# Three tiles of the ConvFFN up projection get other SBUF places: a kernel for one diffusion-transformer layer

## The chip, the cores and the metric

The kernel runs on one core of one Trainium2 chip. The metric is the device time of one execution of the program in microseconds (us). It is compared by the median of several executions.

A few names are used throughout. PE is the matrix engine, DVE the vector engine, ACT the scalar engine, POOL the GpSimd engine, and SP the engine whose queue issues most of the transfers between SBUF (the on-chip memory that all engines read) and DRAM. PSUM is the memory that PE writes its sums to. Each engine works through its own list of instructions in order. An instruction that waits holds up everything behind it on its engine.

## The reference

One layer of a diffusion backbone on 1024 latent tokens of width 1024, in float32. Two attention branches are mixed and added to the residual, a layer norm follows, and then a convolutional feed-forward block. The change lies in the last part, so only that is shown:

```
def _conv_ffn(h, w_up, conv_w, conv_b, w_down):
    u = h @ w_up                                  # (1024 x 1024) @ (1024 x 5632)
    u = depthwise convolution of width 3 along the tokens (u) + conv_b
    gate, val = split(u, 2)                       # 2816 columns each
    return (silu(gate) * val) @ w_down            # (1024 x 2816) @ (2816 x 1024)
...
h = x * (1 + scale2) + shift2
x = layer_norm(DEEPNORM_ALPHA * x + gate2 * _conv_ffn(h, ...))
```

The result must keep float32 accuracy.

## The kernel before, in words

**Layout.** Everything is held transposed: 128 channels on the partitions, the 1024 tokens along the free dimension. Each float32 operand of a large product is split into a high and a low part (`split`, L78: ACT casts the high part, another engine subtracts it for the low part). One product is then three matmuls per 128 channels: high by high, high by low, low by high (`mm3`, L87 to L90).

**Stages.** Modulation and projections come first, then attention, then the output projection with the first layer norm. After that come the up projection with convolution and gating (`up_conv` and `up_tile`), the down projection, and the last layer norm. The up projection has 22 column tiles j of 128 gate and 128 value channels.

**The first three tiles** (j = 0, 1, 2, `NCL = 3`) are done by `up_conv` (L1275) as plain products of the normed activations `B{f}_{half}`. Each gives two PSUM tiles, `u0_j` for the gate and `u1_j` for the values. `conv3` (L1232) turns them into SBUF tiles `c0_j` and `c1_j` with one pass of ACT and two of DVE. ACT applies the Silu to `c0_j` (L1286). `gated` (L1242) multiplies the two on DVE (L1245), forms the sum of the two token halves in the first half of `c1_j` (L1246), and has SP store three pieces to the DRAM tile `td[j]`: the two halves of `c0_j` (L1247, L1248), and the sum from `c1_j`, written twice (L1249).

**The other nineteen tiles** are done by `up_tile` (L1360) with a two-by-two block algorithm that needs seven block products in place of eight (Strassen's form). For tile j these are, in the order in which PE does them: A11 (into bank a), S2 (b), S1 (c), S3 (d), A12 (a), S4 (c), A22 (d). Each is 12 matmuls of 512 columns per bank, so a tile is 84 matmuls. S1 to S4 are sums of weight blocks. The activations need sums too: T1 to T4 (table `prods`, L1228). They are made once, before tile 3, by `build(k)` (L1108) for k = 0 to 3:

- `s1` and `s2` form the sums `t13_k` and `t24_k` in the four-buffer ring `tm`, partly on DVE and partly on POOL
- ACT casts `t13_k` to the high part `T13h_k` and `t24_k` to `T24h_k` (L1115), and DVE makes the low parts `T13l_k` and `T24l_k` (L1116, recorded at the helper's line L1077)

S2 multiplies by T2 and thus by all four `T24h_k` and `T24l_k`, k = 0 to 3 in turn. S1 and S3 use the T13 tiles. In the trace the names have no numbers, so `b<-T24h,wS` is a matmul of S2.

**Where tiles lie.** 35 SBUF places of 4 KB per partition (`H0` to `H18` and `Z0` to `Z15`) are handed out by `ht` (L131) from the front of a list, `hfree`, and given back to its end by `hput` (L135). This happens while the program is written, not while it runs. A place that is given back and taken again makes the new tile's first writer wait until the old tile's last reader is done. Where the old tile is stored to DRAM, that last reader is the transfer, so the wait is for its landing.

**Order of the work.** PE's list is written out by hand in program order. On the other engines a scheduler orders the instructions from the dependences that it sees, so a different place for a tile can move instructions there. The build steps are interleaved with `up_conv` (each waits its turn in the list `pend`).

In `up_conv` before the change, the slot of `c1_j` goes back to the list right after `gated`, while its store is still to come. With the list as short as it is there, these two places are taken again at once:

| Place | Tile before it | Taken next, before | Taken next, after |
|---|---|---|---|
| Z14 | c1_1 (its sum is stored to td[1]) | T24h_2 | tv3 |
| H7 | z1_0 (free early) | T24l_2 | T24h_2 |
| H3 | v1 (free early) | c1_2, then T24h_3 | T24l_2 |
| H18 | z3_0 (read last by build(3)) | T24l_3 | T24h_3 |
| Z2 | v3 (read last by build(3)) | pv3 | T24l_3 |
| Z1 | B3_1 (read by the plain products) | pv4 | c1_2, then pv4 |
| Z12, H17, H5 | B0_1, B1_1, B2_1 | ug3, uv3, tv3 | pv3, ug3, uv3 |

`c1_2` held H3 before, so that `T24h_3` had to wait for the landing of the store of `c1_2`. Later tiles keep the same rotation under other names of places, up to the end of the kernel.

Of the kernel before, what the change touches and what calls it, by code (L numbers as in the profile page):

```python
# [40 lines left out]
NCL = 3  # L41
# [26 lines left out]
def layer_kernel(  # L68
# [59 lines left out]
    hfree = [(hp, f"H{n}") for n in range(19)]  # L128
    hslot = {}

    def ht(name, shape=(P, T), dt=F32):  # L131
        hslot[name] = pool, tag = hfree.pop(0)
        return pool.tile(list(shape), dt, tag=tag, name=name, bufs=1)

    def hput(*names):  # L135
        for n in names:
            hfree.append(hslot.pop(n))
# [741 lines left out]
    def tm(name, dt=F32, w=T):  # L879
        return post.tile([P, w], dt, tag="m", name=name, bufs=4)  # L880
# [22 lines left out]
    def hsl(hf):  # L903
        return slice(hf * HALF, (hf + 1) * HALF)
# [37 lines left out]
    for f in range(2, KT):  # L942
# [4 lines left out]
        for j in range(4):  # L947
            k = (f % 2) * 4 + j
# [59 lines left out]
    def drain(keep=0):  # L1008
        while len(pend) > keep:
            pend.pop(0)[1]()  # L1010
            clock[0] = 0.0
# [64 lines left out]
    def sub(e, o, a, b, op=ALU.subtract):  # L1076
        e.tensor_tensor(out=o, in0=a, in1=b, op=op)  # L1077
# [30 lines left out]
    def build(k):  # L1108
        (b11, b21), (b12, b22) = [[z[:, a] for a in (0, 1)] for z in (zt_[k, 0], tp["v", k])]
        st = {}  # L1110

        def parts(a, e):
            for p in "hl":
                tp[a + p, k] = ht(f"T{a}{p}_{k}", (P, 2, HALF), R32)
            nc.scalar.copy(tp[a + "h", k], st[a])  # L1115
            sub(e, tp[a + "l", k], st[a], tp[a + "h", k].bitcast(F32))  # L1116

        def s1():
            st["13"] = t = tm(f"t13_{k}").rearrange("p (a q) -> p a q", a=2)
            sub(nc.vector, t[:, 1], b12, b11)  # L1120
            sub(nc.gpsimd, t[:, 0], b22, b12)

        def s2():
            st["24"] = t = tm(f"t24_{k}").rearrange("p (a q) -> p a q", a=2)
            sub(nc.vector, t[:, 1], b22, st["13"][:, 1])
            sub(nc.gpsimd if k % 2 else nc.vector, t[:, 0], b21, t[:, 1])
            hput(f"z{k}_0", f"v{k}")

        return [s1, s2, lambda: parts("13", nc.vector), lambda: parts("24", nc.vector)]
# [102 lines left out]
    def conv3(t, u, c):  # L1232
        nc.scalar.activation(t, u, AF.Identity, bias=cvb[:, c:c + 1], scale=cvw[:, c, 1:2])
        nc.vector.scalar_tensor_tensor(out=t[:, 1:T], in0=u[:, 0:T - 1], scalar=cvw[:, c, 0:1], in1=t[:, 1:T],
                                       op0=ALU.mult, op1=ALU.add)
        nc.vector.scalar_tensor_tensor(out=t[:, 0:T - 1], in0=u[:, 1:T], scalar=cvw[:, c, 2:3],
                                       in1=t[:, 0:T - 1], op0=ALU.mult, op1=ALU.add)
# [4 lines left out]
    def gated(j, tg, tv):  # L1242
        lo, hi = tg[:, 0:HALF], tg[:, HALF:T]
        if j < NH:
            nc.vector.tensor_tensor(out=tg, in0=tg, in1=tv, op=ALU.mult)  # L1245
            nc.vector.tensor_tensor(out=tv[:, 0:HALF], in0=lo, in1=hi, op=ALU.add)  # L1246
            nc.sync.dma_start(td[j][:, 0], lo)  # L1247
            nc.sync.dma_start(td[j][:, 3], hi)  # L1248
            nc.sync.dma_start(td[j][:, 1:3], twice(tv[:, 0:HALF]))  # L1249
        else:  # L1250
            nc.vector.scalar_tensor_tensor(out=tg, in0=tg, scalar=-1.0, in1=tv, op0=ALU.mult, op1=ALU.mult)
            nc.sync.dma_start(g2d[j - NH], tg)
            nc.gpsimd.dma_start(td[j - NH][:, 2:4], twice(hi), accum_op=ALU.add)
# [8 lines left out]
    def up_mm(j, gv, slices):  # L1262
        ps, w, done = up_start(j, gv)
        for s in slices:
            if s.start in done:
                continue
            done.add(s.start)
            hf = s.start // HALF
            c = slice(s.start - hf * HALF, s.stop - hf * HALF)
            for k in range(KT):  # L1270
                t = tp["B", k, hf]
                mm3(ps[:, s], (w[0][:, k], w[1][:, k]), (t[:, 0, c], t[:, 1, c]), k == 0, k == KT - 1)
                tick((s.stop - s.start) / 0.8)

    def up_conv(j):  # L1275
        cv = []
        for gv in (0, 1):
            up_mm(j, gv, [hsl(0), hsl(1)])
            if gv == 0:
                hslot[f"c0_{j}"] = pool, tag = cs[j % 2]  # L1280
                t = pool.tile([P, T], F32, tag=tag, name=f"c0_{j}", bufs=1)
            else:
                t = ht(f"c1_{j}")
            conv3(t, ups.pop((j, gv))[0], gv * NF + j)
            cv.append(t)
        nc.scalar.activation(cv[0], cv[0], AF.Silu)  # L1286
        gated(j, *cv)
        hput(f"c1_{j}")

    up_weights(1, 0, 1)  # L1290
    up_weights(1, 1, 1)
# [8 lines left out]
    cs = [hfree.pop(0) for _ in range(2)]  # L1300
    for k in range(4):
        pend += [(BLD, fn) for fn in build(k)]
    for j in range(NCL):
        up_conv(j)
    drain()
    hput(*[f"B{k}_1" for k in range(4)])


    ps3.release()
# [429 lines left out]
```

## Time and profile before

| What | Value |
|---|---|
| Median of 3 runs | 1600.66 us (1598.8 to 1603.46) |
| Profiled execution, its own time | 1605.64 us |
| Its span, first to last instruction | 1603.9 us |
| Time of that execution outside the span | 1.74 us |
| Mean granted clock of PE | 0.991 |
| PE busy | 1538.9 us, 96% of the span |
| DVE, ACT, POOL busy | 74%, 51%, 46% |

The profile is of one execution. Its time of 1605.64 us is 4.98 us over the median of the three runs and 2.18 us over the slowest of them. In a row of the timeline the first number is the start in us from the beginning of the span, the second the length, then engine, line, operation, output and inputs. Brackets at the end give the idle time of the engine just before it and who ended that. The view of waits gives for each pair of instruction and releaser the total wait, how often, and the longest. The view by windows gives busy time of each engine in a stretch, with the granted clock of PE as a share of full speed.

### The profile page before, as it was taken

To read this page: it belongs to the slowest core of one execution; us is meant where nothing else is said; L and a number is where in the kernel's file an instruction comes from. 1 tells how busy PE (TensorE), PEld (TensorE's weight loads), DVE (VectorE), ACT (ScalarE), POOL (GpSimd) and SP (SyncE) were. 2 spreads that over 40 slices of the span, in tenths; PEclk is the share of its full clock that TensorE was granted. 3 is DMA by queue.
4 is the path that set the end of the run, shared out by engine and by line. 5 is a ranking of instruction groups with operands and counts; after the bars stand their busy time and mean duration, and the time that the engine had idled before them with its cause. 6 is when DMAs were issued, how large, how long until landed. Compare 5 with 4: busy or idle time off the path is not lost.

```text
span 1603.9 us, 22190 instructions
## 1 busy us (share of the span) xinstructions
PE 1538.9 (96%) x7748; PEld 1278.2 (80%) x7748; DVE 1180.8 (74%) x1768; ACT 813.6 (51%) x1450; POOL 730.7 (46%) x727
## 2 busy tenths in 40 slices
PE   6999999999998999999999999899999999999997
PEld 5878788888877887777688987688888888888887
DVE  7797646628887777888684788588888788656884
ACT  5422222448887667688431564344544444435552
POOL 0673202426666556665422454366667665021021
PEclk9999999999999999999999999999999999999999
DMA  9695662322236565531451223233334446996831
GB/s 378 225 315 185 199 211 84 118 83 65 61 114 142 137 134 136 122 74 33 164 168 41 79 80 105 93 106 105 105 106 105 106 113 175 354 286 207 260 108 53
DMA packets 112368, 230.00 MB, mean 143 GB/s; under 512 B 12960, under 2 KB 27808, under 8 KB 112160
## 3 DMA queue, kind: packets, MB, share of 16 engines
q1 hardware_dynamic: 96816, 198.93, 37.5%
q0 software_dynamic: 10400, 20.19, 8.3%
q10 hardware_dynamic: 5040, 9.46, 1.6%
q8 instruction: 61, 1.00, 0.3%
q14 instruction: 51, 0.42, 0.1%
HBM read 177.35 MB, written 65.86 MB: 152 GB/s over the span
## 4 chain that ended last, share of the span: by engine, by line
PE 77%; DVE 10%; ACT 4%; DMA 4%; issue 4%; POOL 2%; SPq 0%; DVEq 0%; ACTq 0%; POOLq 0%
PE ptr L529 5%; PE p L88 4%; PE p L89 4%; PE p L90 4%; PE g L88 2%; PE g L89 2%; PE g L90 2%; PE s L412 2%; PE av L550 2%; PE b L90 2%; PE b L89 2%; PE c L88 2%; PE c L89 2%; PE c L90 2%; PE b L88 2%
## 5 line engine op out<-in xcount | busy, mean ns | idle before, releaser
L539 DVE TENSOR_TENSOR ptl<-ptr,pth 128x512 fp32r<-128x512 f32 x188 | 124.6, 684 | 30.0 <-ACT pth L538 27.8
L529 PE MATMUL ptr<-ident,p 128*128 128x128 f32 x816 | 127.7, 279 | 11.6 <-DVE ptl L539 6.8
L538 ACT CAST pth<-ptr 128x512 fp32r<-128x512 f32 x188 | 106.6, 588 | 58.0 <-PE ptr L529 32.8
L85 DVE TENSOR_TENSOR ld<-rd,hd 128x1024 fp32r<-128x1024 f32 x77 | 94.8, 1249 | 50.0 <-ACT hd L80 44.9
L424 ACT ACTIVATE p<-p,nm 128x1024 f32<-128x1024 f32 (+2 forms) x128 | 125.3, 981 | 11.1 <-DVE p L457 10.3
L529 PEld LDWEIGHTS ptr<-ident,p 128*128 128x128 f32 x816 | 94.5, 141 | 42.1 <-DVE ptl L539 13.6
L80 ACT CAST hd<-rd 128x1024 fp32r<-128x1024 f32 x77 | 79.4, 1050 | 81.9 <-PE p L90 55.1
L550 PE MATMUL av<-pth,VT 128*128 128x512 f32 x236 | 104.9, 445 | 1.0 <-ACT avs L556 0.5
L88 PE MATMUL p<-hd 128*128 128x512 f32 x264 | 103.2, 391 | 0.0
L89 PE MATMUL p<-ld,hd 128*128 128x512 f32 x264 | 102.8, 390 | 0.0
L90 PE MATMUL p<-hd,ld 128*128 128x512 f32 x264 | 102.8, 389 | 0.0
L90 PE MATMUL g<-hh,wlg 128*128 128x512 f32 x256 | 99.8, 390 | 0.5 <-POOL wlg L85 0.5
L88 PE MATMUL g<-hh,whg 128*128 128x512 f32 x256 | 99.9, 390 | 0.0
L89 PE MATMUL g<-hl,whg 128*128 128x512 f32 x256 | 99.6, 389 | 0.0
L551 PE MATMUL av<-ptl,VT 128*128 128x512 f32 x236 | 97.8, 415 | 1.8 <-POOL ptl L85 1.8
L85 POOL TENSOR_TENSOR wlg<-wg,whg 128x512 fp32r<-128x512 f32 x32 | 44.1, 1385 | 115.0 <-ACT whg L80 115.0
L457 DVE TENSOR_SCALAR_CACHE_REDUCE p<-s,cvt,nmc 128x1024 f32<-128x1024 f32 x64 | 84.4, 1339 | 12.7 <-PE s L413 12.0
L412 PE MATMUL s<-KL,q 128*128 128x512 f32 (+2 forms) x192 | 76.3, 397 | 2.9 <-ACT p_x L424 2.0
L186 DVE CUSTOM_DVE_ANT_0 wml<-wml,sc,bmc 128x1024 f32<-128x1024 f32 x32 | 47.0, 1478 | 42.7 <-DMA wml<-in_wmodT_dram 40.8
L413 PE MATMUL s<-KL,q 128*128 128x512 f32 (+2 forms) x192 | 71.9, 375 | 0.0
L80 ACT CAST wS<-s 128x512 fp32r<-128x512 f32 x76 | 45.8, 621 | 50.0 <-POOL s L1077 45.8
L82 POOL TENSOR_SCALAR pth<-prw 128x512 fp32r<-128x512 f32 x48 | 31.1, 649 | 87.5 <-ACT prw L535 62.2
(420 smaller groups left out, 4955.9 us busy)
## 6 DMA issues: line engine op xcount, KB each, us to landing
wml<-in_wmodT_dram SPq DMA_DIRECT2D x48, 512.0 KB
ru<-in_w_up_dram SPq DMA_DIRECT2D x38, 512.0 KB
rd<-td SPq DMA_DIRECT2D x55, 256.0 KB
rd<-sd SPq DMA_DIRECT2D x44, 256.0 KB
rd<-in_w_dn_dram SPq DMA_DIRECT2D x33, 256.0 KB
wm<-in_wmodT_dram SPq DMA_DIRECT2D x16, 512.0 KB
wg<-in_w_g_dram SPq DMA_DIRECT2D x32, 256.0 KB
sgd<-sg ACTq DMA_DIRECT2D x32, 256.0 KB
```

The source lines that it names most:

```text
L80: nc.scalar.copy(hi, src)
L85: lo_eng.tensor_tensor(out=lo, in0=src, in1=hi.bitcast(F32), op=ALU.subtract)
L88: nc.tensor.matmul(ps, a[0], b[0], start=start, stop=False, skip_group_check=resumed)
L89: nc.tensor.matmul(ps, a[0], b[1], start=False, stop=False, skip_group_check=resumed)
L90: nc.tensor.matmul(ps, a[1], b[0], start=False, stop=stop, skip_group_check=resumed)
L412: nc.tensor.matmul(o, self.q[0][:, hs], ks, start=True, stop=False)
L424: nc.scalar.activation(p, s, AF.Exp, bias=nm[:, h:h + 1], scale=scale, accum_out=sm[:, h:h + 1])
L529: nc.tensor.transpose(tr[:, h * P:(h + 1) * P], self.pslice(h, n), ident)
L538: nc.scalar.copy(hi, tr)
L539: nc.vector.tensor_tensor(out=lo, in0=tr, in1=hi.bitcast(F32), op=ALU.subtract)
L550: nc.tensor.matmul(self.av, v, hi, start=first, stop=False)
L551: nc.tensor.matmul(self.av, v, lo, start=False, stop=self.left == 0)
```

## The change

It has three edits, all in the placing of tiles. First, before `c1_2` is placed, the place of `B3_1` is given back and put at the front of the list, so that `c1_2` takes it. Second, the places of `c1_1` and `c1_2` aren't given back after `gated`, but after the whole stage. Third, at the end of the stage only `B0_1` to `B2_1` are still given back, and then `c1_1` and `c1_2`. The place of `c1_0` is given back at once as before.

```
             else:
+                if j == NCL - 1:
+                    hput("B3_1")
+                    hfree.insert(0, hfree.pop())
                 t = ht(f"c1_{j}")
...
         gated(j, *cv)
-        hput(f"c1_{j}")
+        if j:
+            later.append(f"c1_{j}")
+        else:
+            hput(f"c1_{j}")
...
+    later = []
     for j in range(NCL):
         up_conv(j)
     drain()
-    hput(*[f"B{k}_1" for k in range(4)])
+    hput(*[f"B{k}_1" for k in range(3)], *later)
```

No instruction is added or removed, and the lists of PE and SP stay as they were. ACT, DVE and POOL get another order in one stretch, the end of `up_conv` and the first steps of tile 3.

ACT before, from the Silu of tile 1's gate to the cast of `T24h_2`. `wS1_3` is the weight operand S1 of tile 3, `s12_3` and `s34_3` are the weight sums that POOL makes, and what an instruction waits for stands in brackets (`DMAHW6` is a transfer queue's count).

```order
L1286 ACTIVATE c0_1_10226<-c0_1_10226 128x1024 [waits DVE_49,Activation_49]
L1115 CAST T13h_3_10461<-t13_3_10455 128x1024 [waits DVE_49,Pool_49]
L1233 ACTIVATE c1_1_10293<-u1_1_10230,cvt_70 128x1024 [waits DMAHW7_49,DMAHW0_49,PE_49]
L80 CAST wS1_3_10497<-s12_3_10485 128x512 [waits Pool_49]
L80 CAST wS2_3_10494<-s12_3_10485 128x512 [waits Pool_49]
L80 CAST wS3_3_10500<-s34_3_10486 128x512 [waits Pool_49]
L80 CAST wA12_3_10551<-ru0_3_10481 128x512 [waits PE_49]
L1233 ACTIVATE c0_2_10372<-u0_2_10309,cvt_70 128x1024 [waits DMAHW2_49,DMAHW1_49,PE_49]
L1115 CAST T24h_2_10432<-t24_2_10404 128x1024 [waits DMAHW6_49,DVE_49,Activation_49]
```

ACT before, a little later, around the cast of `T24h_3`. The row `pv3` is the first copy that follows product A11 of tile 3.

```order
L1233 ACTIVATE c1_2_10445<-u1_2_10382,cvt_70 128x1024 [waits PE_49]
L80 CAST wA11_4_10584<-ru0_4_10560 128x512 [waits DMAHW0_49]
L1368 COPY pv3_10507<-a3_10503 128x512 [waits PE_49]
L80 CAST wS2_4_10617<-s12_4_10564 128x512 [waits Pool_49]
L1115 CAST T24h_3_10465<-t24_3_10458 128x1024 [waits DMAHW3_49,DVE_49,Activation_49]
L80 CAST wS1_4_10620<-s12_4_10564 128x512 [waits PE_49]
```

ACT now, from the same Silu:

```order
L1289 ACTIVATE c0_1_10226<-c0_1_10226 128x1024 [waits DVE_49,Activation_49]
L1115 CAST T24h_2_10432<-t24_2_10404 128x1024 [waits DVE_49]
L1115 CAST T13h_3_10461<-t13_3_10455 128x1024 [waits DVE_49,Pool_49]
L1233 ACTIVATE c1_1_10293<-u1_1_10230,cvt_70 128x1024 [waits DMAHW7_49,DMAHW0_49,PE_49]
L80 CAST wS1_3_10497<-s12_3_10485 128x512 [waits Pool_49]
L1115 CAST T24h_3_10465<-t24_3_10458 128x1024 [waits Pool_49]
L80 CAST wS2_3_10494<-s12_3_10485 128x512 [waits Pool_49]
L80 CAST wS3_3_10500<-s34_3_10486 128x512
L80 CAST wA12_3_10551<-ru0_3_10481 128x512 [waits PE_49]
L1233 ACTIVATE c0_2_10372<-u0_2_10309,cvt_70 128x1024 [waits DMAHW2_49,DMAHW1_49,PE_49]
```

`T24h_2` moves ahead by seven rows and `T24h_3` by eleven, and neither waits for a transfer any more. `T24h_3` waits for POOL alone, that is for the half of `t24_3` that POOL makes.

DVE, the difference from the sum `t13_3` to the low part of the weight operand A11 of tile 3 (`wA11_3`), the first operand that PE needs there:

```order
 L1077 TENSOR_TENSOR t13_3_10455<-v3_9945,z3_0_9083 128x512
+L1077 TENSOR_TENSOR T24l_2_10433<-t24_2_10404,T24h_2_10432 128x1024
+L1077 TENSOR_TENSOR T24l_1_10363<-t24_1_10334,T24h_1_10362 128x1024
+L1234 SCALAR_TENSOR_TENSOR c1_1_10293<-u1_1_10230,cvt_70,c1_1_10293 128x1023
+L1077 TENSOR_TENSOR t24_3_10458<-v3_9945,t13_3_10455 128x512
+L1236 SCALAR_TENSOR_TENSOR c1_1_10293<-u1_1_10230,cvt_70,c1_1_10293 128x1023
+L1077 TENSOR_TENSOR T13l_3_10462<-t13_3_10455,T13h_3_10461 128x1024
+L1245 TENSOR_TENSOR c0_1_10226<-c0_1_10226,c1_1_10293 128x1024
+L1077 TENSOR_TENSOR T24l_3_10466<-t24_3_10458,T24h_3_10465 128x1024
+L1246 TENSOR_TENSOR c1_1_10293<-c0_1_10226 128x512
 L85 TENSOR_TENSOR wA11_3_10491<-ru0_3_10481,wA11_3_10491 128x512
```

Before, `wA11_3` stood right behind `t13_3`. Now nine rows stand between them. Behind `wA11_3` follow the low parts of S2, S1, S3 and A12 of tile 3 in one run, and then the convolution of `c0_2`. Before, `T24l_2` stood inside that convolution, and `T24l_3` behind the low part of tile 4's S2.

On POOL three rows change places: the sums `s12_3` (first half), `s34_3` (first half) and `t24_3` now come in this order, with the second half of `s12_3` after them. Before, both halves of `s12_3` came first, then `t24_3`, then `s34_3`. The first half of `s12_3` waited for DVE's `T24l_1` before and waits for `T24l_2` now, since their `tm` buffers are reused.

Two waits for transfers are new in the later rows: the first writer of `tv3` waits for the store of `c1_1` (its place was Z14), and the copy to `pv4` on ACT waits for the store of `c1_2` (Z1).

## The prediction

> **What bounds the kernel now.** I read the page first, then the view by windows around the end of `up_conv`, the waits there, PE's timeline, and the chain of waits that ends last.
>
> ```profile
> span 1603.9 us, 22190 instructions
> PE 1538.9 (96%) x7748; PEld 1278.2 (80%) x7748; DVE 1180.8 (74%) x1768; ACT 813.6 (51%) x1450; POOL 730.7 (46%) x727
> core 0: us, PE busy (x) PEld busy (x) DVE busy (x) ACT busy (x) POOL busy (x), PEclk, DMA share, GB/s
> 964.00:998.00 34.00, 34.00 (x151) 28.15 (x150) 26.91 (x27) 14.63 (x18) 15.64 (x10) 1.00 0.31 108
> 998.00:1010.00 12.00, 4.54 (x16) 3.11 (x15) 7.03 (x7) 2.33 (x4) 1.54 (x2) 0.83 0.39 131
> 1010.00:1024.00 14.00, 14.00 (x57) 11.36 (x57) 4.07 (x6) 4.76 (x8) 4.72 (x4) 0.90 0.12 39
> 1024.00:1354.00 330.00, 330.00 (x1458) 273.25 (x1457) 279.91 (x252) 159.89 (x226) 219.93 (x127) 1.00 0.40 112
> 1354.00:1550.00 196.00, 196.00 (x869) 161.51 (x868) 136.64 (x141) 97.83 (x107) 36.67 (x29) 1.00 0.82 254
> ```
>
> PE bounds the kernel: it is busy for 96% of the span. From 1024 to 1550 us it has no idle time at all, at full granted clock. In 998 to 1010 it works 4.54 of 12 us, and there and in the next stretch its clock is 0.83 and 0.90. So there is one hole, and whatever closes it moves all behind it ahead. The waits of the stretch 964 to 1024 and the chain name the cause:
>
> ```profile
> POOL s L1077 <- DVE T24l L1077: 15.2, 1, 15.2
> ACT T24h L1115 <- DMA td<-c: 9.7, 2, 6.8
> PE b L88 <- ACT T24h L1115: 7.0, 1, 7.0
> ...
> 996.57 1.11 ACT c L1233
> ...
> 1000.09 1.21 DVE c L1236
> ...
> 1001.32 1.24 DVE c L1245
> ...
> 1003.48 3.22 DMA td<-c
> ...
> 1006.79 1.05 ACT T24h L1115
> ...
> 1007.87 1.24 DVE T24l L1077
> ...
> 1009.15 0.80 PE b L89
> ```
>
> Read upwards: PE's product S2 of tile 3 waits for `T24h_3`, ACT's cast for the landing of `c1_2`'s store out of the same place H3, and that store for the whole convolution of tile 2, which can't start before PE has finished `u1_2`. The operand itself was long ready. Two casts waited for stores: the longer wait, 6.8 us, is `T24h_3`; the other is `T24h_2`, for which PE did not wait.
>
> **What the change takes away.** PE's own rows give the size of the hole:
>
> ```profile
> 995.98 0.39 PE L88 MATMUL a<-B,wA 128*128 128x512 f32 x1
> ...
> 998.70 0.39 PE L88 MATMUL b<-T24h,wS 128*128 128x512 f32 x1
> ...
> 1000.51 0.39 PE L90 MATMUL b<-T24h,wS 128*128 128x512 f32 x1
> 1007.89 0.79 PE L88 MATMUL b<-T24h,wS 128*128 128x512 f32 x1 [6.99 <-ACT T24h L1115]
> 1009.15 0.80 PE L89 MATMUL b<-T24l,wS 128*128 128x512 f32 x1 [0.47 <-DVE T24l L1077]
> ...
> 1011.45 0.63 PE L88 MATMUL c<-T13h,wS 128*128 128x512 f32 x1
> 1011.87 0.63 PE L89 MATMUL c<-T13l,wS 128*128 128x512 f32 x1
> ...
> 1025.07 0.39 PE L88 MATMUL a<-B,wA 128*128 128x512 f32 x1
> ```
>
> - Product A11's 12 matmuls take 998.70 − 995.98 = 2.72 us, so one starts every 0.227 us.
> - Tile 3 begins at 995.98 and tile 4 at 1025.07, which is 29.09 us for 84 matmuls. At 0.227 they take 19.04. The hole costs **10.05 us**.
> - Of these, 7.15 are standing still: the next start would have been 1000.51 + 0.23 = 1000.74, and it came at 1007.89.
> - The other 2.90 come after it: 0.47 of waiting for `T24l_3`, and starts 0.42 us apart (1011.45 to 1011.87) until the granted clock is back.
>
> The clock term rests on those rows. The Trainium skill, "TensorE: Matmul & The Clock Gate", Part 1, says that PE falls to half its clock after an idle window of about 3.4 us and needs as long a busy one to come back. By that page the tail would be 1.7 us (half of 3.4) and the wait of 0.47, so that the hole would be worth about 9.3 us and the estimate would end near 1591.3. I keep the measured 10.05.
>
> **Is the new operand there in time?** The rest depends on when the four moved rows finish now. These rows of before carry the estimate:
>
> ```profile
> 971.97 1.06 ACT L1286 ACTIVATE c<-c 128x1024 f32<-128x1024 f32 x1 [4.83 <-DVE c L1236]
> 974.30 1.05 ACT L1115 CAST T13h<-t 128x1024 fp32r<-128x1024 f32 x1 [1.27 <-DVE t L1077]
> 975.26 1.20 ACT L1233 ACTIVATE c<-u,cvt 128x1024 f32<-128x1024 f32 x1
> 973.53 0.68 DVE L1077 TENSOR_TENSOR t<-v,z 128x512 f32<-128x512 f32 x1
> 975.09 1.23 DVE L1077 TENSOR_TENSOR T24l<-t,T24h 128x1024 fp32r<-128x1024 f32 x1 [0.27 <-DMA td<-c]
> 982.12 2.30 DVE L1245 TENSOR_TENSOR c<-c,c 128x1024 f32<-128x1024 f32 x1
> 987.25 0.68 DVE L85 TENSOR_TENSOR wA<-ru,wA 128x512 fp32r<-128x512 f32 x1
> 976.45 1.62 POOL L1077 TENSOR_TENSOR s<-ru 128x512 f32<-128x512 f32 x1 [15.16 <-DVE T24l L1077]
> 983.30 2.27 POOL L1077 TENSOR_TENSOR s<-ru,s 128x512 f32<-128x512 f32 x1
> ```
>
> ACT ends the Silu at 973.0 and casts `T24h_2` (1.05) by 974.1. DVE makes `T24l_2` by 975.3 and `T24l_1`, whose own store had landed by 975.09, by 976.5. ACT's first pass for `c1_1` still ends near 976.5, since `T13h_3` before it had 1.27 us to wait anyway. DVE then does the first pass of `c1_1` (1.21, as the rows of the chain) and its half of `t24_3` (0.68), to 978.4.
>
> POOL starts `s12_3` at 975.3 instead of 976.45. With 1.62 for each sum it comes to its half of `t24_3` near 978.6 and ends it near 980.2. ACT casts `T24h_3` to 981.3. DVE meanwhile does a pass (1.21), `T13l_3` (1.23) and the product of tile 1 (1.24 as in the chain, 2.30 as measured beside POOL). So `T24l_3` ends near 983.3 to 984.4.
>
> PE first touches that pair at 1000.74. **Spare: about 16 us.** The gain doesn't hang on the reordering being fast.
>
> What is pushed back is `wA11_3`, from behind 973.53 + 0.68 = 974.2 to about 984.7 to 985.8 (two rows of 0.68 further), and four more low parts behind it end near 987 to 988 (the last, A12's, ended at 987.93 before). PE needs `wA11_3` at 995.98: spare 10 us. The convolution of `c0_2` starts where it did, and `T24l_2` no longer stands inside it, so it ends earlier.
>
> One thing speaks against the move: DVE and POOL slow one another. The tile-1 product took 2.30 us with POOL's row of 2.27 beside it, against 1.24 in the chain. The Trainium skill, "SBUF — State Buffer", section "SBUF: two separate sides", says that a DVE operation with two SBUF inputs and a GpSimd operation that reads SBUF exclude one another for a whole instruction. By that page each of POOL's five sums may hold DVE once. If each of the five sums held DVE for 2.27 us, `wA11_3` would end at 985.8 + 11.4 = 997.2, 1.2 us late instead of 10 early. That is the bound, and the row of 2.30 is one measured case, in which about 1 us was lost. I take none of it for the sum.
>
> **The two new waits.** `tv3` now waits for `c1_1`'s store, issued at 986.79 in the first row below. It is needed when tile 3 ends, at 995.98 + 19.04 = 1015.0. `pv4`'s copy on ACT waits for `c1_2`'s store. Behind it stand the casts for tile 5, so this is the one to watch:
>
> ```profile
> 986.79 0.37 SPq L1249 DMA_DIRECT2D td<-c  x1
> 1029.19 0.57 ACT L1368 COPY pv<-a 128x512 f32<-128x512 f32 x1
> ```
>
> The copy ran at 1029.19; 10.05 earlier is 1019.1. The store lands at 1003.48 + 3.22 = 1006.7, as its convolution still follows `u1_2`. So 12.4 us are spare, and the wait costs nothing. If that cover were gone, tile 5's S2 operand would be late, and PE uses it from 995.98 + 2 × 19.04 + 2.72 = 1036.8 on, another 17 us later.
>
> `c1_2` in `B3_1`'s place needs PE to have read `B3_1`. That is done within the same PSUM tile `u1_2` whose last matmul it needs anyway, so it adds nothing. SP's and PE's lists are the same, so no transfer is moved past another.
>
> **The sum.** 1605.64 − 10.05 = 1595.6 us for an execution like the profiled one. That one lies 4.98 over the median. The hole is a chain of fixed pieces, so I take the same 10.05 off the median: 1600.66 − 10.05 = **1590.6 us**. A difference of 0.3%, 4.8 us, is about what a measurement of this kernel can tell from none.
>
> **The rivals.**
>
> - *Part of the hole stays (chance 0.05).* The reason would be DVE and POOL holding one another as above, or `T24l_3` later than PE. For: DVE gets nine rows in a row there. Against: 10 us spare. With half of the 10.05 left the time is 1600.66 − 5.0 = 1595.6, still faster.
> - *No difference (0.06).* The down projection, 1354 to 1550, gives the gain back, because its transfers, not PE, set its pace: the DMA share there is 0.82. If their start didn't move with PE, PE would wait there for 10 us, and the time is 1600.7. Against: PE has 196.00 of 196 us busy there, and loads start when a buffer comes free, which moves along. That the change doesn't do what it says would end here too, but no wait of the T24 casts for a store is left.
> - *Slower (0.04).* `T24h_3` comes late for another reason, and `wA11_3`, now behind `T24l_3` on DVE, comes late with it, so that PE stops at 995.98 already. The place would be POOL's half of `t24_3`, behind two sums that wait for the weights of tile 3. If the cast starts at X, `wA11_3` ends at about X + 3.65 (1.05 + 1.24 and two rows of 0.68). The old loss is reached at a wait of 7.15 us, so it decides from X = 995.98 + 7.15 − 3.65 = 999.5. With the old X of 1006.79 the wait is 14.5, 7.3 us more than before, and the time is 1608.0. Against: X is near 980.2, and the weights were there at 976.45, when the first of these sums ran.
>
> **How the numbers follow.** The forecast has 0.85. Its own range is the spread of the runs less 10.05: 1598.8 to 1603.46 gives 1588.75 to 1593.4. With the partial case the range is 1588.5 to 1596.0, which leaves out the other two, 0.10, and a little of each side. Faster is 0.85 + 0.05 = 0.90, same 0.06, slower 0.04.
>
> **What the profile after would show.** Right: no wait of ACT's T24h casts for a store. PE's product S2 of tile 3 runs through, tile 3 takes 19.0 to 19.1 us from its first A11 matmul to tile 4's, and the granted clock is 1.00 from 964 to 1550. `T24l_3` ends before 990, `wA11_3` before 995.98. ACT's copy to `pv4` waits for PE, not for the store. Wrong: PE idle before A11 of tile 3, or a new wait of PE behind 1024, above all in the down projection, or the same tile times and the same total.

## The result and the profile after

| | Before | After |
|---|---|---|
| Median, 6 runs each | 1602.65 us (1598.8 to 1604.43) | 1591.06 us (1587.89 to 1593.3) |
| Ratio, 95% interval | | 0.9931 (0.9917 to 0.9945) |
| Profiled execution, its own time | 1605.64 us | 1593.3 us |
| Its span | 1603.9 us | 1591.5 us |

The ratio means 0.0069 × 1602.65 = 11.1 us less, with 8.8 to 13.3 as the interval. Predicted were 10.05 us and a time of 1590.6.

The page and the view by windows of the kernel after. The windows are the ones of before, except that the last two end 10 us earlier.

```profile
span 1591.5 us, 22189 instructions
PE 1537.1 (97%) x7748; PEld 1278.4 (80%) x7748; DVE 1181.3 (74%) x1768; ACT 813.3 (51%) x1450; POOL 730.1 (46%) x727
...
964.00:998.00 34.00, 34.00 (x151) 28.16 (x151) 29.32 (x27) 13.92 (x18) 16.77 (x11) 1.00 0.30 106
998.00:1010.00 12.00, 12.00 (x54) 9.94 (x54) 6.40 (x9) 3.46 (x6) 3.82 (x4) 1.00 0.52 176
1010.00:1024.00 14.00, 14.00 (x64) 11.59 (x63) 12.55 (x12) 7.88 (x11) 8.49 (x5) 1.00 0.15 51
1024.00:1344.00 320.00, 320.00 (x1414) 265.05 (x1413) 270.58 (x243) 154.38 (x218) 213.38 (x124) 1.00 0.40 115
1344.00:1540.00 196.00, 195.78 (x872) 161.56 (x871) 137.06 (x142) 98.89 (x108) 36.01 (x29) 1.00 0.81 255
```

In 998 to 1010 PE was busy for 4.54 us with a granted clock of 0.83. It is now busy for all 12 us at 1.00. Every engine has as many instructions as before. In the down projection, 1344 to 1540, PE has 195.78 of 196 us busy with the transfers at a share of 0.81 (196.00 and 0.82 before).

The waits of the kernel after, 964 to 1024 us, those that answer to the three of before:

```profile
POOL s L1077 <- DVE T24l L1077: 14.1, 1, 14.1
ACT T24h L1115 <- POOL t L1077: 2.6, 1, 2.6
ACT pv L1375 <- PE a L90: 0.7, 1, 0.7
```

The last row is the copy to `pv3`. The copy to `pv4`, which has the new wait for `c1_2`'s store, is this row of ACT's timeline:

```profile
1016.68 0.57 ACT L1375 COPY pv<-a 128x512 f32<-128x512 f32 x1
```

The row of ACT's T24h casts waiting for a store is gone, and so is PE's row. One cast waits for POOL's half of `t24_3` instead, as the order of the instructions said. ACT's copy to `pv3` waits for PE alone, and the copy to `pv4` for nothing. POOL's 14.1 us and ACT's 2.6 stand off PE's path: PE has no idle time in this stretch.

PE's timeline after, the starts of product A11 and S2 of tile 3 and of A11 of tile 4:

```profile
993.52 0.39 PE L88 MATMUL a<-B,wA 128*128 128x512 f32 x1
...
996.24 0.39 PE L88 MATMUL b<-T24h,wS 128*128 128x512 f32 x1
...
998.74 0.39 PE L90 MATMUL b<-T24h,wS 128*128 128x512 f32 x1
...
1012.56 0.39 PE L88 MATMUL a<-B,wA 128*128 128x512 f32 x1
```

Tile 3 takes 1012.56 − 993.52 = 19.04 us, where it took 29.09. From there to the end of the span it is 1591.5 − 1012.56 = 578.9, and before 1603.9 − 1025.07 = 578.8. So the span's 12.4 us are 10.05 in tile 3, and 995.98 − 993.52 = 2.46 ahead of it. Those 2.46 are not the change's. These rows, the first of before and the second of after, end the same wait of PE in `up_conv`:

```profile
953.64 0.38 PE L89 MATMUL u<-B,hwu 128*128 128x256 f32 x1 [2.88 <-DVE B L1077]
950.65 0.58 PE L89 MATMUL u<-B,hwu 128*128 128x256 f32 x1 [2.87 <-DVE B L1077]
```

The kernel after is 2.99 us ahead there already, of which 2.46 are left at tile 3, and the first instruction in another place, the cast of `T24h_2`, runs only at 969.93. In the profiles of this study tile 3 begins between 988.3 and 996.0, on average at 991.4 in the four kernels in which `T24h_3` waits for `c1_2`'s store and at 991.4 in the six in which it doesn't. The spans of one profile each would have credited the change with a quarter too much. The tile's own length doesn't have that fault.

### The profile page after: what moved, and what is told of

It reads as the page before. It is cut to its first block, busy times and chain, and to the rows that moved or that the text cites. A ratio compares the mean times of both kernels' runs of the same rounds, so it can differ in the third digit from the quotient of the medians.

```text
span 1591.5 us, 22189 instructions
## 1 busy us (share of the span) xinstructions
PE 1537.1 (97%) x7748; PEld 1278.4 (80%) x7748; DVE 1181.3 (74%) x1768; ACT 813.3 (51%) x1450; POOL 730.1 (46%) x727
## 4 chain that ended last, share of the span: by engine, by line
PE 76%; DVE 8%; DMA 7%; ACT 4%; issue 3%; POOL 2%; SPq 0%; DVEq 0%; ACTq 0%; POOLq 0%
PE ptr L529 4%; PE p L89 3%; PE p L88 3%; PE p L90 3%; PE b L90 3%; PE b L89 3%; PE b L88 3%; PE g L88 2%; PE g L89 2%; PE g L90 2%; PE d L89 2%; PE c L89 2%; PE a L89 2%; PE c L90 2%; PE a L90 2%
```

## The experiments

**Theory.** The whole gain is one wait: the cast of `T24h_3` under the pending store of `c1_2`, which PE stood still for. **Rivals.** (A) Freeing `T24h_2` of `c1_1`'s store, or the new order on DVE and ACT, has a part in it. (B) Any store over a T24 place does the harm. (C) The new wait of `pv4`, or a later store, eats a part of the gain. (D) The slow clock behind the wait is no piece of its own but a share of the wait.

"Tile 3" below is the time from its first A11 matmul to tile 4's, 29.09 before and 19.04 after.

### Each hold alone

Only `c1_2` is held back until the stage's end, and `c1_1` given back at once as before:

```
-        if j:
+        if j == NCL - 1:
             later.append(f"c1_{j}")
```

> Only the third tile's edit: c1_2 takes the place of B3_1 and is held to the end of the stage, while c1_1 gives its place back at once as before, so that T24h_2 again waits for the store of c1_1. Theory (the whole gain is T24h_3 no longer waiting for the store of c1_2): ratio to before 0.993 to 0.994, about 10 us less. From tile 3's first A11 matmul to tile 4's 19.0 to 19.1 us, and ACT's wait of T24h_2 for a store is back at about 3 us with nobody on PE waiting for it. Rival (the freed ACT queue of T24h_2 and the shorter DVE list carry part of it): tile 3 takes 21 us or more and the gain is 4 to 8 us.

Only `c1_1` is held, and `c1_2`, which still lies in `B3_1`'s place, is given back at once. `T24h_3` then takes that place:

```
-        if j:
+        if j == 1:
             later.append(f"c1_{j}")
```

> Only the second tile's edit: c1_1 is held to the end of the stage, so that T24h_2 and T24l_2 lie in free places and are made early, but c1_2 gives its place (that of B3_1) back at once and T24h_3 takes it under the pending store. Theory: no gain, ratio 0.998 to 1.002; tile 3 takes 29 us again, with a PE wait of about 7 us for ACT's T24h_3 and a slow clock behind it. Rival (the T24h_2 part counts): a gain of 2 us or more, tile 3 at 27 us or less.

The first ran at 0.9927 (0.9911 to 0.9944) with tile 3 at 19.04, the second at 1.0001 (0.9991 to 1.0012) with tile 3 at 29.89. In the first, the cast of `T24h_2` does wait for its store, as a row of its ACT timeline shows:

```profile
985.10 1.05 ACT L1115 CAST T24h<-t 128x1024 fp32r<-128x1024 f32 x1 [3.29 <-DMA td<-c]
```

It ends at 986.2. PE's S2 follows the first A11 matmul (990.48) by 2.72 us, at 993.2, and sees nothing of it. The second kernel's chain and PE's timeline show the old hole in the new place:

```profile
999.22 3.21 DMA td<-c
```

```profile
995.71 0.39 PE L90 MATMUL b<-T24h,wS 128*128 128x512 f32 x1
1003.63 0.80 PE L88 MATMUL b<-T24h,wS 128*128 128x512 f32 x1 [7.53 <-ACT T24h L1115]
1004.88 0.80 PE L89 MATMUL b<-T24l,wS 128*128 128x512 f32 x1 [0.46 <-DVE T24l L1077]
```

Standing is 1003.63 − 995.71 − 0.23 = 7.69, and the remaining 29.89 − 19.04 − 7.69 = 3.16 come behind it. Rival A falls: one hold has all of the gain, and the other has none that can be measured.

### Another store over the same operand

`T24h_3` goes under a store again, but under the one of `c1_1`: its place is given back when `c1_2` has been placed, and `c1_2` stays held.

```
                 if j == NCL - 1:
                     hput("B3_1")
                     hfree.insert(0, hfree.pop())
                 t = ht(f"c1_{j}")
+                if j == NCL - 1:
+                    hput("c1_1")
...
-        if j:
+        if j == NCL - 1:
             later.append(f"c1_{j}")
-        else:
+        elif j == 0:
```

> T24h_3 is put under a pending store again, but under that of c1_1 (Z14) instead of that of c1_2, with c1_2 in the place of B3_1. Theory (what costs is not a store over the place but one that follows PE's own last product before): the store of c1_1 lands near 987 to 990, PE needs the pair at about 998 to 1001, so the wait is there on ACT (1 to 4 us) and PE doesn't see it: ratio 0.993 to 0.994, tile 3 at 19.0 to 19.1 us. Rival (any wait of a T24 cast for a store holds up ACT and DVE enough for PE to stop): tile 3 over 20 us, gain under 8 us.

It ran at 0.994 (0.9923 to 0.9956), tile 3 at 19.04, and the cast waited on ACT:

```profile
986.65 1.05 ACT L1115 CAST T24h<-t 128x1024 fp32r<-128x1024 f32 x1 [2.05 <-DMA td<-c]
```

PE needs it 4.76 us after tile 3's start (1000.74 − 995.98 before), at 993.78 + 4.76 = 998.5. Rival B falls. Of the two stores only the one that follows PE's last plain product is late enough to matter.

### The least edit

The kernel before with one thing changed: the place of `c1_2` is given back at the stage's end. `c1_2` stays in H3, `c1_1` is not held, and `T24h_3` lies in H18.

```
-        hput(f"c1_{j}")
+        if j < NCL - 1:
+            hput(f"c1_{j}")
...
-    hput(*[f"B{k}_1" for k in range(4)])
+    hput(*[f"B{k}_1" for k in range(4)], "c1_2")
```

> The smallest form of the third tile's edit: the kernel before, with nothing changed but that c1_2 keeps its place (H3) to the end of the stage. B3_1 is not touched, c1_1 gives its place back at once. T24h_3 then lies in H18. Theory (all that matters is that T24h_3 does not lie under the store of c1_2): ratio 0.992 to 0.995, tile 3 at 19.0 to 19.1 us, T24h_2 waits about 3 us for the store of c1_1 with nobody on PE behind it. Rival (the place of B3_1 is needed, since the sums of k = 3 in H18 and Z2 come free late): PE waits for a T24 tile of k = 3 by 1 us or more.

It ran at 0.9934 (0.9914 to 0.9955), tile 3 at 19.04. The cast of `T24h_2` waited 2.97 us for the store of `c1_1`, and PE didn't stop. `B3_1`'s place for `c1_2` isn't needed for the gain either. The intervals of this kernel, of the first one and of the changed kernel overlap, so none is shown to be the fastest.

### The new wait without its cover

In the changed kernel `pv4` lies where `c1_2` was, with 12.4 us to spare by the prediction. Here `pv3` takes that place, whose copy is the first that frees a bank in tile 3:

```
-    hput(*[f"B{k}_1" for k in range(3)], *later)
+    hput("c1_2", *[f"B{k}_1" for k in range(3)], "c1_1")
```

> The changed kernel, but pv3 in place of pv4 takes the place of c1_2, so that the first copy of tile 3 on ACT waits for the store of c1_2. This moves the new wait 19 us nearer. Theory: the store lands near 1004 (issue about 1000.8 and 3.2 us), PE needs bank a again for A12 at about 1004.4, so the copy is done 0.3 to 1.0 us too late: tile 3 takes 19.3 to 20.5 us, ratio 0.993 to 0.995. Rival (a wait at the head of ACT's queue holds up all casts behind it and costs several us): tile 3 or 4 over 21 us.

It ran at 0.9945 (0.9925 to 0.9964), with tile 3 at 20.97, a little over the range. The ACT row, then the chain's row of the store, and then PE's rows where bank a is needed again for A12:

```profile
1003.38 0.58 ACT L1375 COPY pv<-a 128x512 f32<-128x512 f32 x1 [8.44 <-DMA td<-c]
```

```profile
999.18 4.10 DMA td<-c
```

```profile
1001.99 0.39 PE L90 MATMUL d<-T13h,wS 128*128 128x512 f32 x1
1004.02 0.50 PE L88 MATMUL a<-B,wA 128*128 128x512 f32 x1 [1.64 <-ACT pv L1375]
1004.35 0.39 PE L89 MATMUL a<-B,wA 128*128 128x512 f32 x1
1004.58 0.40 PE L90 MATMUL a<-B,wA 128*128 128x512 f32 x1
```

ACT waits 8.44 us, and PE starts 1004.02 − 1001.99 − 0.23 = 1.80 late. The store took 4.10 us in place of the 3.2 counted on, which is the excess. The starts behind it are 0.23 to 0.33 apart at once, and only 1.93 − 1.80 = 0.13 more is lost. So the new wait would cost about 2 us if it stood where PE needs the copy, and in the changed kernel it doesn't. There the copy to `pv4` runs at 1016.68 right behind ACT's work before it, and waits for nothing.

### A later store

Two more stores of `c0_2`, 512 KB each, to spare DRAM tiles `xd` go ahead of `c1_2`'s on SP's list, in the kernel before and in the changed one:

```
+    xd = [dpool.tile([P, T], F32, tag=f"xd{n}", name=f"xd{n}") for n in range(2)]
...
+            if j == NCL - 1:
+                for n in range(2):
+                    nc.sync.dma_start(xd[n], tg)
             nc.sync.dma_start(td[j][:, 1:3], twice(tv[:, 0:HALF]))
```

> The kernel before, with two extra stores of c0_2 (512 KB each, to DRAM tiles that nobody reads) issued ahead of the store of c1_2. Theory (PE's hole ends with the landing of that store): the store lands later by the time of 1 MB, an estimate of 3.5 us from 1 MB in about 4.1 us for the three stores of this tile before; PE's wait grows from 7.0 to 9.5 to 11.5 us and the kernel is slower by 2.5 to 4.5 us, ratio 1.0015 to 1.003. Rival (the cast is late for the DVE pass and the order of the list, the store is only what ends a little later): the wait grows by under 1 us.

> The changed kernel with the same two extra stores. Theory: nobody on PE's path waits for that store any more, and it lands near 1008, 9 us ahead of the copy to pv4: time as the changed kernel, ratio to before 0.992 to 0.995, tile 3 at 19.0 to 19.1 us. Rival (the wait for the store has only moved to the copy to pv4, with little to spare): tile 4 or 5 longer than 19.2 us and the gain smaller by 2 us or more.

The kernel before with them ran at 1.0022 (1.0011 to 1.0034), tile 3 at 32.42. The changed one ran at 0.9945 (0.9927 to 0.9964) against the unloaded kernel before, tile 3 at 19.04. Chain and PE's timeline of the first:

```profile
998.06 4.84 DMA td<-c
```

```profile
993.90 0.39 PE L90 MATMUL b<-T24h,wS 128*128 128x512 f32 x1
1004.10 0.79 PE L88 MATMUL b<-T24h,wS 128*128 128x512 f32 x1 [9.81 <-ACT T24h L1116]
1005.36 0.79 PE L89 MATMUL b<-T24l,wS 128*128 128x512 f32 x1 [0.47 <-DVE T24l L1078]
```

Counted from tile 3's start (989.36 here), the store lands at 13.54 in place of 10.72, 2.82 us later. PE stands still 1004.10 − 993.90 − 0.23 = 9.97 us in place of 7.15, which is 2.82 more. So the old kernel pays for a later landing in full. The rest of tile 3's 32.42 − 29.09 = 3.33 us comes behind the wait. The changed one pays nothing there, and its copy to `pv4` at 1012.12 still waits for nothing. Rival C falls with this and the run before it.

### A shorter wait

To see what the clock costs, the wait is shortened: the kernel before without the two DVE passes in the convolution of `c1_2`. So a part of the convolution of tile 2's values is not computed.

```
     def conv3(t, u, c):
         nc.scalar.activation(t, u, AF.Identity, bias=cvb[:, c:c + 1], scale=cvw[:, c, 1:2])
+        if c == NF + NCL - 1:
+            return
```

> The kernel before, with the two DVE passes of the convolution of c1_2 left out (the values of tile 2 are then only scaled and biased, so part of the convolution is not computed). The store of c1_2 is issued about 3.6 us earlier (two passes of about 1.2 and the row of 1.18 between them). Theory (a standing part that ends with the landing of the store, and a slow clock behind it that comes whole or not at all): PE's standing part shrinks from 7.15 to 3 to 4 us, and the tail behind it stays at 2 to 3.4 us, or is gone (under 0.3 us) if the wait is then too short to lose the clock; ratio 0.996 to 0.999. Rival (the tail is in proportion to the wait): a tail of 1.2 to 1.7 us.

The chain of this kernel, and then PE's timeline:

```profile
994.41 4.04 DMA td<-c
```

```profile
993.76 0.39 PE L90 MATMUL b<-T24h,wS 128*128 128x512 f32 x1
999.65 0.79 PE L88 MATMUL b<-T24h,wS 128*128 128x512 f32 x1 [5.50 <-ACT T24h L1115]
1000.91 0.80 PE L89 MATMUL b<-T24l,wS 128*128 128x512 f32 x1 [0.47 <-DVE T24l L1077]
```

The wait became less short than expected, since the store took 4.04 us and the DVE product ahead of it 2.18 in place of 1.24:

```profile
990.96 2.18 DVE L1247 TENSOR_TENSOR c<-c,c 128x1024 f32<-128x1024 f32 x1 [5.23 <-ACT c L1233]
```

Tile 3 is 27.13, so the hole is 8.09: 5.66 standing (999.65 − 993.76 − 0.23) and 2.43 behind it. The time was 1.0003 (0.999 to 1.0017), which is outside the 0.996 to 0.999 expected and doesn't show the 2 us by which tile 3 is shorter in the profile. The profiled execution was the fastest of the ten (1597.81, with a median of 1601.71). Where the 2 us went in the others stays open. On rival D this run says little by itself: 2.43 lies inside what the theory expected, and a fixed share of the wait would give 5.66 / 7.15 × 2.90 = 2.30. The five holes together say more:

| Kernel | PE stands still, us | Lost behind it, us | of that, waiting for `T24l_3` |
|---|---|---|---|
| `pv3` under the store | 1.80 | 0.13 | none |
| shorter wait | 5.66 | 2.43 | 0.47 |
| before | 7.15 | 2.90 | 0.47 |
| second hold alone | 7.69 | 3.16 | 0.46 |
| before, later store | 9.97 | 3.41 | 0.47 |

Without the wait for `T24l_3` the loss is 1.96, 2.43, 2.70 and 2.94 for waits of 5.66 to 9.97. A share of 2.43 / 7.15 would give 1.92 for 5.66 and 2.61 for 7.69, close to what was measured. But it would give 3.39 for the longest and 0.61 for the shortest wait, and 2.94 and 0.13 were measured. So these five don't fit a fixed share: almost nothing for a wait of 1.80, about 2 us at 5.66, and 1 us more at 9.97. This rests on one profile of each kernel, so how the loss grows among the four long waits is not shown. Where between 1.80 and 5.66 it sets in wasn't tried.

## Why the prediction was right

**The hole.** The step that carried everything, 29.09 − 19.04 = 10.05 us, came out to the hundredth, in the changed kernel and in four others in which `T24h_3` is free of that store in time. Both of its pieces went, 7.15 of standing and 2.90 behind it. The time fell by 11.1 with an interval of 8.8 to 13.3, which holds 10.05. That the time came within 0.5 us of the 1590.6 has luck in it: the forecast started from the 1600.66 of three runs, and over six runs the kernel before had 1602.65.

**The clock term.** I kept the measured 2.90. The four long waits bear that out with 2.43 to 3.41 behind each, and the changed kernel gained all of its 2.90. PE's starts were back at full pace 4.0 us (shorter wait) to 6.1 us (before, later store) after the first of them behind the wait, the stop for `T24l_3` included. The estimate from the Trainium skill, "TensorE: Matmul & The Clock Gate", Part 1, 1.7 with the measured wait of 0.47 added, is less than any of the four losses. The time of the runs can't tell 10.05 from the 9.3 that this estimate makes of the hole, since both lie between 8.8 and 13.3. Tile 3's length can. The Trainium skill says there too that the window in which activity is watched runs free, so that the number of slow matmuls changes from run to run. One profile of each kernel can't show how much of the spread is that.

**The new operand in time.** These rows of ACT, DVE and POOL in the kernel after answer to the walk through the moved instructions:

```profile
969.93 1.04 ACT L1115 CAST T24h<-t 128x1024 fp32r<-128x1024 f32 x1
977.90 1.05 ACT L1115 CAST T24h<-t 128x1024 fp32r<-128x1024 f32 x1 [2.62 <-POOL t L1077]
977.54 1.41 DVE L1077 TENSOR_TENSOR T13l<-t,T13h 128x1024 fp32r<-128x1024 f32 x1
978.87 2.31 DVE L1245 TENSOR_TENSOR c<-c,c 128x1024 f32<-128x1024 f32 x1
981.10 2.31 DVE L1077 TENSOR_TENSOR T24l<-t,T24h 128x1024 fp32r<-128x1024 f32 x1
983.93 0.68 DVE L85 TENSOR_TENSOR wA<-ru,wA 128x512 fp32r<-128x512 f32 x1
984.53 2.98 DVE L85 TENSOR_TENSOR wS<-s,wS 128x512 fp32r<-128x512 f32 x3
987.43 0.68 DVE L85 TENSOR_TENSOR wA<-ru,wA 128x512 fp32r<-128x512 f32 x1
976.57 1.29 POOL L1077 TENSOR_TENSOR t<-z,t 128x512 f32<-128x512 f32 x1 [0.69 <-DVE t L1077]
977.82 2.28 POOL L1077 TENSOR_TENSOR s<-s,ru 128x512 f32<-128x512 f32 x1
980.18 2.15 POOL L1077 TENSOR_TENSOR s<-ru,s 128x512 f32<-128x512 f32 x1
```

With 2.46 added, to stand on the clock of before, the cast of `T24h_3` starts at 980.36 (predicted 980.2). `T24l_3` ends at 983.41 + 2.46 = 985.87 (predicted 983.3 to 984.4), `wA11_3` at 987.07 (984.7 to 985.8), and A12's low part at 990.57 (987 to 988). The first is right, though not by the pieces that were added up: POOL began 0.4 us earlier than counted on, and its half of `t24_3` then stood 0.69 waiting for DVE's. From there on DVE's list is 1.3 to 3.6 us late, because POOL held it more often than in the one row that I went by. I took none of that for the sum, and it was indeed none: `wA11_3` ended at 984.61, and PE needed it at 993.52, so 8.9 of the 10 us of spare were left.

**The rivals.** That part of the hole stays: it needed over 10 us of delay on DVE, and `wA11_3` was 1.3 to 2.4 late. That the down projection gives the gain back: from the first matmul of the down projection it took 1591.5 − 1355.3 = 236.2 us to the end of the span, and 1603.9 − 1367.8 = 236.1 before. Its transfers moved along with PE, although their share is 0.81. Slower: the point X = 999.5 for the cast of `T24h_3` was missed by 19 us. The spare of `pv4` was real: its copy ran at 1016.68 + 2.46 = 1019.1, as predicted, and waited neither for the store nor, as I had listed among the signs, for PE. The first writer of `tv3`, at 1014.07, waited only for DVE. The experiment that took the spare of `pv4` away shows what such a wait costs without it: 2 us, not the old 10.

**What was off.** The size of the contention of DVE and POOL, and it ended inside the spare. Of the three edits one carries the gain: that the place of `c1_2` isn't handed on at once.

## What to carry to other kernels

Before handing a buffer on, ask whether its last reader is a transfer, and what stands between that transfer's issue and the new owner's use. Here a store that was issued after the last product that PE had left made the next writer wait for the whole landing, and PE needed the newly written tile before that. Give the freed place to a tile that is written late, and measure the gain by the length of the stage, not by the span of one execution.

## What the hardware showed beyond that

**DVE and POOL took turns.** In the rows above POOL's sum that starts at 977.82 takes 2.28 us, where the same size took 1.29 just before (976.57). DVE's `T13l` runs until 978.95, and the sum ends at 980.10, 1.15 later. DVE's product, listed from 978.87, ends at 981.18, which is 1.08 after that. POOL's next sum ends at 982.33, 1.15 later, and DVE's `T24l` at 983.41, 1.08 later. Each row spans the other engine's turn and its own, so in such a run both engines work at about half pace. The Trainium skill, "SBUF — State Buffer", section "SBUF: two separate sides", says that of a DVE operation with two SBUF inputs and a GpSimd operation that reads SBUF, the one that starts first has the shared ports for its whole instruction and the other is blocked. The rows agree, with 2.31 for an instruction of 1.24.

**`c1_2`'s store took 3.2 to 4.8 us to land.** 3.22 before and 3.21 with the second hold alone, 4.10 with `pv3` under it, 4.04 with the shorter wait, and 4.84 with 1 MB more ahead of it. Why the third and fourth were slower isn't known. Whoever lets an instruction wait for such a landing should count on a spread like that.
